# Moving a 32-byte constant and widening another so that SBUF buffers start on 64-byte lines

## The chip, the cores and the metric

The kernel runs on one core of one Trainium2 chip. The metric is device time in microseconds (us) from one launch; smaller is better. A core has a matrix engine (PE in the profile, with its weight loads shown as PEld), a vector engine (DVE), a scalar engine (ACT), a general engine (POOL) and a queue engine that issues most transfers (SP). On-chip data lie in SBUF, 128 partitions with the same layout in each, so an address here is a byte offset within a partition. Sums of matrix products lie in PSUM.

## The reference

The reference is a two-layer block for a latent generator: 512 latent tokens and 256 context tokens, model width 1024, 16 heads of 64. Every layer is a mixer and then a SwiGLU feed-forward network of hidden width 2816, each behind an RMS norm whose shift, scale and gate come from a conditioning vector.

```python
for l in range(DEPTH):                      # DEPTH = 2
    mx = (s_c @ mod_w[l] + mod_b[l]); mc = (s_cc @ mod_w[l] + mod_b[l])   # 6 vectors each
    hx = _rms(x, norm_mix_w[l]) * (1.0 + scx1) + shx1                     # the same for ctx
    if l % 2 == 0: ax, ac = _even_mixer(...)    # windowed and dense grouped-query attention
    else:          ax, ac = _odd_mixer(...)     # difference of two softmaxes per head
    x = x + gx1 * ax
    x = x + gx2 * _swiglu(_rms(x, norm_ffn_w[l]) * (1.0 + scx2) + shx2, ffn_w_in[l], ffn_w_out[l])
    # not in the last layer: the same two updates of ctx
return x
```

Everything is float32.

## The kernel before

**Arithmetic.** A large product of float32 matrices is made of three products of float32r operands: each operand is split into a rounded high part (a CAST on ACT, for instance L901) and a low part, the difference (a subtraction on DVE or POOL, for instance L911). High times high, high times low and low times high are summed in PSUM. A matrix multiplication on PE has a stationary operand of 128 columns, loaded first, and a moving operand of up to 512 columns that streams past it.

**Stages, in order.** The start loads modulation weights and makes the first norm (0 to 35 us). Layer 0's mixer follows: the input projection (`inps`, L466 to L468), scores (`sc`, L578), transposed probabilities (`ppt`, L612), values (`av`, L623) and the output projection (`ops`, L807 to L809). Layer 0's first feed-forward product (`p` and `pz`, L933) works on blocks of 384 tokens; its second one (`dps`, L1030 to L1032) has 512 moving columns. Layer 1 has the same shape with other attention lines (L715, L716, L734, L744), its feed-forward product works on blocks of 256 tokens, also on L933, and its second one is L1076 to L1078. The modulation sums of later parts run between the products of layer 0's feed-forward network (`modrow` L245, `modcol` L252).

**What the feed-forward product on L933 does.** The weights are the stationary operand (`wbh`, `wbl`) and the tokens the moving one. It is a block scheme with seven products a step, each of 12 matmuls. The moving blocks are `hT` (B11, B21), `b` (B12, B22, T4), `t` (T1, T3) and `hTt` (T2).

**Order.** From the sixth attention step of layer 0 on, PE's order is the one written in the source (`manual_schedule`); the other engines' orders, and PE's before that step, are laid out by a planner that simulates the program's time.

**Where buffers lie.** Pools stack up in SBUF from two ends, the left (low addresses) and the right (the top). Each tile's size is rounded up to a multiple of 32 bytes. In the allocation that the program before carries:

| side | first address, in bytes | pools |
|---|---|---|
| left | 16,512 (a multiple of 64) | cp (constants), keep, small, start, mix0, odd0, even0, blk0, rawh0, mods0, out0, state0 to 2, mix1, hid_low, hid_high, ring1, hop1, tmp1, g2 |
| right | top at 229,344 (32 past a multiple of 64) | mw0, w0, opa, blkt0, ring0, tmp0, mods1, wt, whi, wlo, mw1, w1 |

In `cp`, the tile `cst` has 262 columns of 4 bytes, 1,048 bytes, which occupy 1,056 (16.5 times 64). So `identr`, `identb`, `maskb` and `neghalf` behind it begin 32 bytes past a multiple of 64; `neghalf` has 32 bytes, and from `cols` on the left side is on multiples of 64 again. Only tiles of a few bytes in `small`, in `cp`'s tail and `negsink` fall on odd multiples of 32 there. On the right every size is a multiple of 64, so with the top 32 past a line every right tile begins 32 bytes past one.

A tile that begins on a multiple of 64 is called even in this document, one that begins 32 bytes behind it odd. The large operands are then:

| matmuls | moving | stationary |
|---|---|---|
| `inps` L466 to L468 | `wih`, `wil`, `wihi`, `wilo` in mw0, whi, wlo: odd | `hT`, `hTc` in keep: even |
| `sc` L578, L715, L716 | `kT` in even0, odd0, state: even | `qt`: even |
| `ops` L807 to L809 | `woh`, `wol` and most `wo` in w0, w1: odd; `wo` in keep: even | `hT`, `hTc`: even |
| layer 0, L933 | `hT`, `b`, `hTt`: even; `t` in blkt0: odd | `wbh`, `wbl` in ring0: odd |
| layer 0, L1030 to L1032 | even | even |
| layer 1, L933 and L1076 to L1078 | even | even |

The lines that the change touches are these:

```python
C_N = C_S4 + 4                                            # L42
cp = es.enter_context(tc.tile_pool(name="cp", bufs=1))    # L71
neghalf = cp.tile([P, 8], F32, name="neghalf")            # L139
```

`cst` is loaded once, by the first transfer of the queue (L121). `neghalf` is the exponent of the reciprocal square roots on POOL (L160), of at most 5 columns, and the input of two activations (L1360, L1740).

Of the kernel before, what the change touches and what calls it, by code (L numbers as in the profile page):

```python
# [11 lines left out]
F32 = mybir.dt.float32  # L12
# [7 lines left out]
P = 128  # L20
# [18 lines left out]
LAM_INIT = 0.8 - 0.6 * math.exp(-0.3)  # L39

C_ID, C_S2, C_ONE, C_S4 = 0, 128, 130, 258
C_N = C_S4 + 4  # L42


def swap_pairs(ap):
# [18 lines left out]
def backbone(es: ExitStack, tc: tile.TileContext, x, c, ctx, c_ctx, mod_w, mod_b, norm_mix_w, norm_ffn_w,  # L64
# [3 lines left out]
    nc = tc.nc  # L68
    PSUM = bass.MemoryType.PSUM

    cp = es.enter_context(tc.tile_pool(name="cp", bufs=1))  # L71
    keep = es.enter_context(tc.tile_pool(name="keep", bufs=1))
    small = es.enter_context(tc.tile_pool(name="small", bufs=6))
    dram = es.enter_context(tc.tile_pool(name="dram", bufs=1, space=bass.MemoryType.DRAM))
# [44 lines left out]

    cst = cp.tile([P, C_N], F32, name="cst")  # L120
    nc.sync.dma_start(cst, consts)  # L121
# [14 lines left out]
    mk = start.pool.tile([P, 2, P], F32, name="mk")  # L136
    nc.scalar.dma_start(mk, masks)
    nc.scalar.copy(maskb, mk)
    neghalf = cp.tile([P, 8], F32, name="neghalf")  # L139
    nc.gpsimd.memset(neghalf, -0.5)  # L140

    nc.scalar.activation(rows[0:16, :], rows[0:16, :], AF.Silu)
# [1105 lines left out]
    if True:  # L1248
        for i, (b, t) in enumerate(steps):
# [11 lines left out]
            if b < 3:  # L1261
                n = QUARTS[b][j]
# [571 lines left out]
def _constants():  # L1834
    k = np.zeros((P, C_N), np.float32)
    p = np.arange(P)
    k[:, C_ID:C_ID + P] = np.eye(P)
    k[:, C_S2] = p % 32 == 0
    k[:, C_S2 + 1] = p % 32 == 1
    k[:, C_ONE:C_ONE + P] = 1.0  # L1840
    k[:, C_S4:] = p[:, None] == 32 * np.arange(4)
    t = np.arange(SEQ)
    nf = HD // 4
    inv = np.float32(THETA) ** (-np.arange(nf, dtype=np.float32) / np.float32(nf))
    ang = np.concatenate([(t // GRID_W).astype(np.float32)[:, None] * inv,
                          (t % GRID_W).astype(np.float32)[:, None] * inv], axis=-1).astype(np.float32)
    cos, sin = np.cos(ang), np.sin(ang)
    r = np.empty((SEQ, 2, HD), np.float32)
    r[:, 0] = np.repeat(cos, 2, axis=-1)
    r[:, 1, 0::2] = -sin  # L1850
    r[:, 1, 1::2] = sin
    r = np.ascontiguousarray(r.reshape(NTX, P, 2, HD).transpose(1, 0, 2, 3))
    m = np.empty((P, 2, P), np.float32)
    m[:, 0] = np.where(p[None, :] >= p[:, None], 0.0, NEG)
    m[:, 1] = np.where(p[None, :] <= p[:, None], 0.0, NEG)
    return {"consts": k, "masks": m, "rope": r}
# [31 lines left out]
```

## Time and profile before

| what | value |
|---|---|
| median of 3 runs | 1697.88 us (1696.89 to 1704.94) |
| the profiled execution's own time | 1699.53 us |
| its span, first to last instruction | 1697.7 us |
| PE busy, share of the span | 1638.4 us, 97% |
| mean granted clock of PE | 0.993 |
| DVE, ACT, POOL busy | 1145.6, 939.1, 700.8 us |

The page gives busy time by engine and by line. The view of instructions in order of time gives a start and a length for each matmul. Matmuls overlap, and their ends are modelled, so what one costs in a full stream is the distance from its start to the next one's start, and not the length shown.

### The profile page before, as it was taken

The page shows a single profiled execution, that of the slowest core. Times are in us where ns is not written, and L with a number is a line of the kernel's source. Part 1 is how long each engine was busy: PE and PEld are TensorE (multiplying, and loading weights), DVE is VectorE, ACT ScalarE, POOL GpSimd, SP SyncE. Part 2 cuts the span into 40 slices and gives each one's busy share as a digit, 9 for nine tenths or more (in the row PEclk, how much of TensorE's full clock was granted, in tenths as well). Part 3 has the DMA queues.
Part 4 walks back from the last instruction along what each step waited for, and adds up shares of the span by engine and source line. Part 5 has one row for each costly group of instructions (what it writes and reads, how often), then busy time and mean ns, then how long its engine had stood idle before and what let it go on. Part 6 is the DMA issues. An engine that isn't in the chain of part 4 may idle for free. (4 is left out here: it accounts for less than half of the span.)

```text
span 1697.7 us, 28553 instructions
## 1 busy us (share of the span) xinstructions
PE 1638.4 (97%) x10378; PEld 1474.3 (87%) x10378; DVE 1145.6 (67%) x2012; ACT 939.1 (55%) x2011; POOL 700.8 (41%) x867
## 2 busy tenths in 40 slices
PE   6999999899999999999999989999999999999998
PEld 3977777677999999998777889999988899999887
DVE  3765656744899887767767656666666598887433
ACT  5565565745455665545564456666666555555321
POOL 2765554311345554402413366666664242221000
PEclk8999999999999999999999999999999999999999
DMA  9222221511455554439955311111112433331431
GB/s 323 65 71 75 69 69 50 180 45 48 120 168 174 171 158 150 136 115 330 309 185 177 104 41 38 48 44 42 46 47 99 122 91 106 107 106 57 137 98 63
DMA packets 217964, 194.64 MB, mean 115 GB/s; under 512 B 20000, under 2 KB 202592, under 8 KB 217824
## 3 DMA queue, kind: packets, MB, share of 16 engines
q1 hardware_dynamic: 217472, 192.62, 36.8%
q8 instruction: 81, 1.33, 0.3%
q14 instruction: 59, 0.48, 0.1%
q10 hardware_dynamic: 352, 0.21, 0.0%
HBM read 179.91 MB, written 12.87 MB: 114 GB/s over the span
## 5 line engine op out<-in xcount | busy, mean ns | idle before, releaser
L901 ACT CAST wbh<-wr 128x512 fp32r<-128x512 f32 x170 | 104.7, 621 | 139.2 <-PE p L933 76.0
L933 PE MATMUL p<-hT,wbh 128*128 128x256 f32 (+1 forms) x752 | 154.8, 299 | 0.0
L911 POOL TENSOR_TENSOR wbl<-wr,wbh 128x512 fp32r<-128x512 f32 x43 | 58.7, 1365 | 174.8 <-ACT wbh L901 174.8
L933 PEld LDWEIGHTS p<-hT,wbh 128*128 128x128 f32 x752 | 121.9, 191 | 0.2
L911 DVE TENSOR_TENSOR wbl<-wr,wbh 128x512 fp32r<-128x512 f32 x127 | 105.9, 842 | 22.9 <-ACT wbh L901 19.6
L933 PE MATMUL p<-hT,wbl 128*128 128x256 f32 (+1 forms) x376 | 112.1, 298 | 0.0
L933 PE MATMUL p<-t,wbh 128*128 128x384 f32 (+1 forms) x480 | 111.0, 317 | 0.0
L604 POOL TENSOR_SCALAR Pt<-Pt,rc 128x256 f32<-128x256 f32 (+3 forms) x96 | 73.3, 776 | 87.6 <-DVE rc L601 80.1
L231 POOL TENSOR_TENSOR modp<-modp 128x512 f32<-128x512 f32 x40 | 57.0, 1424 | 120.4 <-ACT modp L230 112.8
L933 PE MATMUL p<-hTt,wbh 128*128 128x256 f32 (+1 forms) x480 | 101.3, 303 | 0.0
L887 POOL TENSOR_TENSOR wr<-wr 128x512 f32<-128x512 f32 x40 | 61.7, 1543 | 85.3 <-DVE ws L892 84.3
L466 PE MATMUL inps<-wih,hT 128*128 128x384 f32 x256 | 90.6, 354 | 6.4 <-ACT qkv L677 6.4
L933 PE MATMUL p<-b,wbh 128*128 128x384 f32 x368 | 94.7, 339 | 0.3 <-DVE c L961 0.3
L901 ACT CAST wbh<-ws 128x512 fp32r<-128x512 f32 x120 | 69.6, 581 | 42.0 <-PE p L933 29.1
L224 DVE SCALAR_TENSOR_TENSOR ma<-modw,cols,ma 128x256 f32<-128x256 f32 x140 | 86.3, 617 | 2.3
L592 ACT ACTIVATE Pt<-sc,nm 128x256 f32<-128x256 f32 (+3 forms) x96 | 67.8, 709 | 35.1 <-DVE nm L588 19.1
L468 PE MATMUL inps<-wih,hT 128*128 128x384 f32 x256 | 86.7, 339 | 0.0
L467 PE MATMUL inps<-wil,hT 128*128 128x384 f32 x256 | 86.5, 338 | 0.0
L911 DVE TENSOR_TENSOR wbl<-ws,wbh 128x512 fp32r<-128x512 f32 x120 | 81.6, 680 | 2.1 <-ACT wbh L901 2.0
L933 PEld LDWEIGHTS p<-t,wbh 128*128 128x128 f32 x480 | 82.9, 189 | 0.0
L933 PEld LDWEIGHTS p<-hTt,wbh 128*128 128x128 f32 x480 | 78.4, 191 | 3.1 <-ACT modp L230 2.1
L230 ACT ACTIVATE modp<-modw,cols 128x256 f32<-128x256 f32 x160 | 68.4, 500 | 15.6 <-DMA modw<-in_mod_w_dram 7.7
(355 smaller groups left out, 5378.8 us busy)
## 6 DMA issues: line engine op xcount, KB each, us to landing
modw<-in_mod_w_dram SPq DMA_DIRECT2D x96, 512.0 KB, 4.5
wr<-in_ffn_w_in_dram SPq DMA_DIRECT2D x176, 256.0 KB, 3.4
wdr<-in_ffn_w_out_dram SPq DMA_DIRECT2D x66, 512.0 KB, 3.7
wir<-in_od_w_in_dram SPq DMA_DIRECT2D x96, 128.0 KB, 2.3
hidm<-hid SPq DMA_DIRECT2D x44, 192.0 KB, 1.9
hr<-hidm SPq DMA_DIRECT2D x22, 192.0 KB, 3.4
x<-in_x_dram SPq DMA_DIRECT2D x8, 512.0 KB, 6.1
wir<-in_ev_w_in_dram SPq DMA_DIRECT2D x16, 256.0 KB
```

Of the source, the lines that this page charges most:

```text
L224: nc.vector.scalar_tensor_tensor(acc, w[:, k], scale[k], acc, ALU.mult, ALU.add)
L230: nc.scalar.activation(pr[:, k], w[:, k], AF.Copy, scale=scale[k])
L231: nc.gpsimd.tensor_add(pr[:, 0:2], pr[:, 0:2], pr[:, 2:4])
L466: nc.tensor.matmul(ps, hs[0][:, k, :], a, start=k == 0, stop=False)
L467: nc.tensor.matmul(ps, hs[0][:, k, :], b, start=False, stop=False)
L468: nc.tensor.matmul(ps, hs[1][:, k, :], a, start=False, stop=k == KT - 1)
L592: turn["exp"] = nc.scalar.activation(p[:, :n], s, AF.Exp, bias=nm[:, c1], accum_out=sm[:, c1])
L604: nc.gpsimd.tensor_scalar(p[:, :n], p[:, :n], rc[:, hh:hh + 1], 1.0, ALU.mult, ALU.mult)
L887: nc.gpsimd.tensor_sub(w, raw[f, "G1"], w)
L901: nc.scalar.copy(hi, w)
L911: (nc.gpsimd if name == "G2" else nc.vector).tensor_sub(lo, raw[need[n]], f32(hi))
L933: nc.tensor.matmul(ps, w[:, k, :], H[b][h][:, k, :], start=first and k == 0 and q == 0, stop=final and k == 3 and q == 2, skip_group_check ...
```

## The change

`cst` gets eight more columns of zeros (its rows go from 1,048 to 1,080 bytes, which occupy 1,088, 17 times 64), and `neghalf` goes into a pool of its own, `edge`, which is opened first on the right side and so takes the top 32 bytes. The left side from `cols` on stays where it was, since 32 bytes come and 32 go; `identr`, `identb` and `maskb` move up by 32 to a multiple of 64. The right side's pools all move down by 32, to multiples of 64. No instruction is added, removed or given another shape but the load of `cst`.

```diff
 C_ID, C_S2, C_ONE, C_S4 = 0, 128, 130, 258
-C_N = C_S4 + 4
+C_N = C_S4 + 12
...
-    cp = es.enter_context(tc.tile_pool(name="cp", bufs=1))
+    cp, edge = (es.enter_context(tc.tile_pool(name=n, bufs=1, side=s)) for n, s in (("cp", "left"), ("edge", "right")))
...
-    neghalf = cp.tile([P, 8], F32, name="neghalf")
+    neghalf = edge.tile([P, 8], F32, name="neghalf")
     nc.gpsimd.memset(neghalf, -0.5)
...
-    k[:, C_S4:] = p[:, None] == 32 * np.arange(4)
+    k[:, C_S4:C_S4 + 4] = p[:, None] == 32 * np.arange(4)
```

## The prediction

> **What bounds the kernel now.** I read the page's busy times first, then the busy time of each engine by stage, then the instructions of PE in order of time, and the chain that ended last.
>
> ```profile
> span 1697.7 us, 28553 instructions
> PE 1638.4 (97%) x10378; PEld 1474.3 (87%) x10378; DVE 1145.6 (67%) x2012; ACT 939.1 (55%) x2011; POOL 700.8 (41%) x867
> ```
>
> ```profile
> 100.00:410.00 310.00, 294.89 (x2049) 234.29 (x2049) 187.51 (x399) 182.02 (x430) 133.63 (x198) 0.99 0.25 78
> 410.00:840.00 430.00, 429.22 (x2386) 407.21 (x2385) 341.12 (x544) 236.85 (x461) 178.39 (x143) 1.00 0.57 176
> 1000.00:1270.00 270.00, 262.33 (x1813) 251.65 (x1812) 171.85 (x350) 174.86 (x452) 180.55 (x285) 1.00 0.14 42
> 1348.00:1573.00 225.00, 225.00 (x1877) 224.94 (x1876) 190.31 (x284) 127.43 (x245) 63.78 (x45) 1.00 0.34 97
> ```
>
> The second fence has, for a stretch of time, its length and the busy time of PE, weight loads, DVE, ACT and POOL, then the granted clock. PE bounds every large stage: it idles 0.8 of 430 us in layer 0's feed-forward part, nothing in layer 1's, 7.7 of 270 us in layer 1's mixer and 15 of 310 us in layer 0's. So only what shortens PE's stream counts, and the question is what an address has to do with the distance between two matmuls.
>
> **Where PE's distance depends on parity.** A full stream is seen best where all buffers are even, in layer 1's feed-forward product:
>
> ```profile
> 1376.16 1.44 PE pz L933 x12
> 1377.60 8.64 PE p L933 x72
> 1386.24 1.44 PE pz L933 x12
> ```
>
> 72 matmuls of 256 columns take 8.64 us, 120.0 ns each. In layer 0 the same line has 384 columns; its stationary `wbh` and `wbl` are odd, its moving blocks even except `t`:
>
> ```profile
> 605.80 0.51 PE L933 MATMUL p<-b,wbh 128*128 128x384 f32 x2
> 607.36 0.51 PE L933 MATMUL p<-t,wbh 128*128 128x384 f32 x2
> 609.27 0.34 PE L933 MATMUL p<-t,wbl 128*128 128x384 f32 x1
> 609.44 0.50 PE L252 MATMUL modcol<-cst,ma 128*128 128x4 f32 x4
> 614.05 0.52 PE L933 MATMUL p<-b,wbh 128*128 128x384 f32 x2
> 616.17 0.52 PE L933 MATMUL p<-hTt,wbh 128*128 128x384 f32 x2
> ```
>
> From 605.80 to 607.36 lie nine matmuls: 173.3 ns each. From 607.36 to 609.27, on `t`, eleven: 173.6. But from 614.05, right behind another `t` block, twelve matmuls on the same `b` take 2.12 us, 176.7 each. The first pace is the full one: 173.3 minus 120.0 over 128 columns is 0.417 ns a column, which leaves 13.3 ns a matmul and gives 226.7 for 512 columns. The second is 3.4 ns slower, and stays so until something else breaks the stream. I followed all even-moving stretches of this product by their starts. 32 begin right behind a `t` block, and every one is slow; 20 begin elsewhere (behind modulation matmuls, at the product's start), and none is. The first and the last slow one:
>
> ```profile
> 464.25 0.34 PE L933 MATMUL p<-hTt,wbh 128*128 128x384 f32 x1
> 470.62 0.51 PE L933 MATMUL p<-t,wbh 128*128 128x384 f32 x2
> ...
> 750.21 0.52 PE L933 MATMUL p<-b,wbh 128*128 128x384 f32 x2
> 752.33 0.27 PE L288 MATMUL gps<-cst,modc 128*8 128x128 f32 x1
> ```
>
> They are 36 matmuls in 6.37 us (176.9) and 12 in 2.12 (176.7). The other two products of mixed parity have an odd moving and an even stationary operand:
>
> ```profile
> 1053.04 0.34 PE L466 MATMUL inps<-wih,hT 128*128 128x384 f32 x1
> 1055.16 0.27 PE L734 MATMUL ppt<-cst,e 128*128 128x128 f32 x1
> ```
>
> ```profile
> 360.90 0.39 PE L807 MATMUL ops<-woh,hT 128*128 128x512 f32 x1
> 366.27 0.40 PE L809 MATMUL ops<-woh,hT 128*128 128x512 f32 x1
> ```
>
> `inps`: twelve in 2.12 us, 176.7 against 173.3. `ops`: 23 in 5.37 us, 233.5 against 226.7, 6.8 too many, and no faster at the end than at the start. An all-even product of 512 columns that is entered badly recovers:
>
> ```profile
> 904.62 0.40 PE L1030 MATMUL dps<-wdh,hdh 128*128 128x512 f32 x1
> 906.47 0.39 PE L1032 MATMUL dps<-wdh,hdl 128*128 128x512 f32 x1
> 908.50 0.39 PE L1032 MATMUL dps<-wdh,hdl 128*128 128x512 f32 x1
> ```
>
> Eight matmuls at 231, then nine at 226. My reading: where moving and stationary operand have the same parity (`t` with `wbh`, all of layer 1's product, `dps`) PE falls into the full pace; where they differ, a slow pace, once entered, lasts.
>
> **The change, part by part.** All these operands become even, so the slow pace should go.
>
> ```profile
> L466 PE MATMUL inps<-wih,hT 128*128 128x384 f32 x256 | 90.6, 354 | 6.4 <-ACT qkv L677 6.4
> L466 PE MATMUL inps<-wihi,hT 128*128 128x384 f32 x128 | 47.1, 368 | 0.3 <-ACT qkv L520 0.3
> L466 PE MATMUL inps<-wihi,hTc 128*128 128x384 f32 x64 | 23.3, 364 | 1.1 <-ACT qkv L520 1.1
> L807 PE MATMUL ops<-wo,hT 128*128 128x512 f32 x64 | 26.5, 413 | 0.0
> L807 PE MATMUL ops<-woh,hT 128*128 128x512 f32 x64 | 25.5, 398 | 0.0
> L807 PE MATMUL ops<-woh,hTc 128*128 128x512 f32 x32 | 12.8, 401 | 0.0
> ```
>
> Layer 0's product: 780 of its matmuls lie in the 32 slow stretches; times 3.4 ns is 2.7 us. The ceiling is all 1,344 even-moving ones, 4.6. The stage is full of PE, so all of it counts. It waits for no transfer there, so where those land in SBUF is hidden.
>
> `inps`: 448 on L466 and as many on L467 and L468, 1,344 times 3.4 is 4.6 us. What stays is a bad entry, some 112 of them (one for each 12). A `dps` entry costs 8 times 4.6 ns, 36 ns; half of that for 384 columns leaves 2.0 us, while the clean entries behind modulation matmuls leave nothing. I take 1.0, so 3.6 saved.
>
> `ops`: 160 on each of three lines; 72 of the 480 have the even `wo` in `keep`. 408 times 6.8 is 2.8 us; 20 entries of 36 ns stay, 0.7, so 2.1 saved.
>
> The last two stand in the mixers, where PE idles 3 to 5% and waits for ACT's copies (first row above); I count 90%, 5.1 us of 5.7.
>
> The other operands. The scores' 192 or so matmuls of 512 columns are even already, but run between `inps` blocks; they may start cleaner, 0 to 6.8 ns each, 0 to 1.3 us; I take 0.4, as they are runs of four, shorter than the recovery seen. The 368 float32r transposes (`identr`, `qd`, `kd`) go from two odd operands to two even ones; by `t` against layer 1 that is nothing, and I allow 0.4 us of at most 1.3 (3.4 ns each). The load of `cst` grows by 4 KB, 0.013 us at the 324 GB/s of the start:
>
> ```profile
> 0.00:35.00 35.00, 20.89 (x154) 12.46 (x154) 11.34 (x27) 20.60 (x39) 6.71 (x19) 0.95 0.98 324
> ```
>
> For ACT, DVE and POOL nothing: the same cast on odd buffers (layer 0) and on even ones (layer 1) takes the same time, and what they gain or lose hides behind PE in both stages.
>
> ```profile
> L901 ACT CAST wbh<-wr 128x512 fp32r<-128x512 f32 x86 | 53.0, 621 | 87.1 <-PE p L933 46.2 <-issue 38.8 <-DMA wr<-in_ffn_w_in_dram 1.5
> ...
> L901 ACT CAST wbh<-wr 128x512 fp32r<-128x512 f32 x84 | 51.7, 620 | 52.1 <-PE p L933 29.8 <-PE pz L933 11.2 <-ACT s L938 11.1
> ```
>
> `neghalf`, 32 bytes, is written and read as before. No wait is added: a tile waits for earlier ones in its place, and after the move the pairs that share an address are those of before, less three that shared 32 bytes and whose first tile was long dead.
>
> Sum: 2.7 + 5.1 + 0.4 + 0.4 = 8.6 us. The profiled execution took 1699.53 us with 1.8 outside its span; the median of the runs is 1697.88. From the median, 1689.3; from the profiled execution, 1690.9.
>
> [...]
>
> **The rivals.** *No change.* The slow pace could hang on something that goes with the order, the size of matmul before or the PSUM bank, and not on parity. For it: the scores are even and not at the full pace. Against it: 32 of 32 and 0 of 20, with the same operands. Time 1697.9.
>
> *More.* Every entry becomes clean as well: 2.7 + 4.6 + 2.8 + 1.3 + 1.3 is 12.7 us, 1685.2. For it: entries behind modulation matmuls are clean. Against it: `dps` at 904.62 is even and enters badly.
>
> *Slower.* The planner lays out ACT, DVE, POOL and the queue by simulated time, and `cst`'s load is the first event. If it moves one of ACT's copies behind a cast at every head of layer 1, PE waits there:
>
> ```profile
> PE inps L466 <- ACT qkv L677: 4.3, 8, 1.3
> ```
>
> That is eight waits and 4.3 us now. Four more such sums eat the gain and make 17 us, from which it would be over 0.5% slower, 1706.4. Against it: nothing in an engine's work changes, and 4 KB shift all events alike.
>
> **How the numbers follow.** The forecast, a gain of 4.5 to 11 us around 8.6, has 0.74, half of it above 8.5 us (0.5% of 1697.88, about what a measurement of this kernel can tell from no change). More has 0.11, no change 0.08, slower 0.07. Faster by over 0.5% is then 0.37 + 0.11, 0.48; within 0.5% is 0.37 + 0.08, 0.45; slower 0.07. The forecast's own range is 1687 to 1693; with More at the low end and a mixer that gives back most of its share at the high one (2.7 us of the first part alone gives 1695.2), 1684.5 to 1695.5 holds 0.8.
>
> **What would show it.** In the view of instructions in order of time, `b` and `hTt` behind `t` at 173.3 ns and not 176.7; twelve `inps` in 2.08 us; `ops` behind its first eight at 226.7; layer 0's feed-forward part 2.7 us shorter, layer 1's unchanged. It is wrong if those distances stay, if the orders of ACT or POOL differ, or if PE's waits grow by what its stream loses.

## The result, and the profile after

The kernel after takes 1695.45 us (median of 22 runs, 1691.36 to 1698.70), the kernel before 1699.44 us over 22 runs beside it (1694.96 to 1704.94). The ratio is 0.9974, with a 95% interval of 0.9966 to 0.9983: a gain of 4.4 us, between 2.9 and 5.8 (the two medians lie 4.0 apart). The forecast was a gain of 8.6, in a range of 4.5 to 11. The direction was right; what was measured is half of what was forecast, just under that range. The change stays within the 0.5% that the prediction took for what a measurement can tell, but over 22 runs the interval is only 0.09% to either side and leaves no change out.

The page of the kernel after, its span and its line of busy times:

```profile
span 1690.7 us, 28553 instructions
PE 1628.1 (96%) x10378; PEld 1465.3 (87%) x10378; DVE 1143.5 (68%) x2012; ACT 938.4 (56%) x2011; POOL 695.1 (41%) x867
```

This profiled execution took 1692.5 us, that of before 1699.53. Their difference, 7.0 us, is more than the medians show: the execution of after lies 3 us below its own median, that of before at its median. Part of it is therefore not the change's. The mean granted clock, 0.993 before and 0.995 after, stands for some 3.4 us of it, an estimate (0.7% of 1697.7 us less 0.5% of 1690.7; in before, where the clock is 0.50 from 1272.6 us on for 3.4 us, two scores of 512 columns start 0.43 us apart, and 0.24 behind it). The same instructions stand in the same order on every engine as before, so stages can be compared one by one.

The busy time by stage of the kernel after (length, then PE, weight loads, DVE, ACT and POOL, then the granted clock):

```profile
100.00:410.00 310.00, 293.99 (x2061) 234.17 (x2060) 189.30 (x403) 182.22 (x431) 134.45 (x201) 1.00 0.25 79
410.00:840.00 430.00, 429.02 (x2391) 407.05 (x2390) 340.58 (x546) 238.55 (x463) 183.37 (x145) 1.00 0.57 179
1000.00:1270.00 270.00, 260.78 (x1827) 249.91 (x1826) 173.91 (x353) 176.62 (x458) 178.44 (x286) 1.00 0.15 44
1348.00:1573.00 225.00, 225.00 (x1851) 223.78 (x1850) 192.87 (x285) 127.16 (x244) 61.59 (x42) 1.00 0.34 99
```

PE still fills both feed-forward parts (429.02 of 430 us, 225.00 of 225). In layer 1's mixer, though, it now idles 9.2 of 270 us (7.7 before), and in layer 0's 16.0 of 310 (15.1 before): part of what PE's stream gave up there has come back as waiting.

What became of the stretches behind `t` shows in the instructions in order of time, of the kernel after:

```profile
612.58 0.51 PE L933 MATMUL p<-t,wbh 128*128 128x384 f32 x2
...
613.10 0.50 PE L933 MATMUL p<-b,wbh 128*128 128x384 f32 x2
...
615.17 0.51 PE L933 MATMUL p<-hTt,wbh 128*128 128x384 f32 x2
```

Twelve matmuls on `b` behind a `t` block take 2.07 us, 172.5 ns each, where they took 176.7: the slow pace that the prediction rests on is gone there. But another has appeared. Behind a modulation sum, before and after:

```profile
508.67 0.64 PE L245 MATMUL modrow<-ma,cst 128*32 128x256 f32 x8
...
511.42 0.51 PE L933 MATMUL pz<-hT,wbh 128*128 128x384 f32 x2
...
513.50 0.51 PE L933 MATMUL p<-b,wbh 128*128 128x384 f32 x2
...
515.58 0.34 PE L933 MATMUL p<-t,wbh 128*128 128x384 f32 x1
```

```profile
508.13 0.64 PE L245 MATMUL modrow<-ma,cst 128*32 128x256 f32 x8
...
510.90 0.51 PE L933 MATMUL pz<-hT,wbh 128*128 128x384 f32 x2
...
513.00 0.51 PE L933 MATMUL p<-b,wbh 128*128 128x384 f32 x2
...
515.10 0.51 PE L933 MATMUL p<-t,wbh 128*128 128x384 f32 x2
```

From 511.42 to 515.58 lie 24 matmuls before, 4.16 us, 173.3 ns each; from 510.90 to 515.10 the same 24 after, 4.20 us, 175.0. These stretches were clean before. Counted as unbroken runs of even-moving matmuls, 19 stretches of this product don't begin behind `t` (20 by the prediction's count), and all are clean before. In after, the seven behind `modrow` are slow by 1.3 ns a matmul, the three behind the transposes `gps` by 3.5, and the two at the product's start by 1.8 and 2.8; the seven behind `modcol` stay clean.

`inps` and `ops` of the kernel after (one mixed block each; the rows between are left out):

```profile
1056.64 0.34 PE L467 MATMUL inps<-wil,hT 128*128 128x384 f32 x1
...
1058.55 0.47 PE L696 MATMUL qpt<-identr,qd 128*128 128x128 f32 x4
```

```profile
361.07 0.40 PE L807 MATMUL ops<-woh,hT 128*128 128x512 f32 x1
...
366.34 0.39 PE L809 MATMUL ops<-woh,hT 128*128 128x512 f32 x1
```

Eleven `inps` take 1.91 us, 173.6 ns each (176.7 before). 23 `ops` take 5.27 us, 229.1 (233.5 before, 226.7 forecast). And PE's wait at the head of the `inps` blocks, in the view of waits of the kernel after (microseconds, times, longest):

```profile
PE inps L466 <- ACT qkv L677: 8.6, 11, 1.4
```

It was 7.2 over the same 11 times.

**Stages over all traces.** Since one trace holds some microseconds of chance, I measured four stages in the traces of every kernel below that computes the block, from the first matmul of one stage to the first of the next. For the kernels before and after, the rows that bound layer 0's `ops` and feed-forward stages:

```profile
332.44 0.40 PE L807 MATMUL ops<-woh,hT 128*128 128x512 f32 x1
...
425.89 0.33 PE L933 MATMUL p<-hT 128*128 128x384 f32 x1
...
763.46 0.40 PE L1030 MATMUL dps<-hT,hTt 128*128 128x512 f32 x1
```

```profile
332.86 0.39 PE L807 MATMUL ops<-woh,hT 128*128 128x512 f32 x1
...
425.45 0.34 PE L933 MATMUL p<-hT 128*128 128x384 f32 x1
...
761.88 0.39 PE L1030 MATMUL dps<-hT,hTt 128*128 128x512 f32 x1
```

The table gives them all, under the names of the experiments below. "Distance" is the place of the large right-hand tiles minus that of the left-hand ones, modulo 128 bytes, in `inps` and in the other two; it turned out to be the better name for what is varied than even and odd.

| kernel | distance (`inps`; `ops` and L933) | layer 0's mixer, `sc` to `ops` | `ops` stage, layer 0 | L933, layer 0 | layer 1's mixer, `sc` to `ops` |
|---|---|---|---|---|---|
| before | 96; 96 | 259.61 | 93.46 | 337.57 | 265.03 |
| e2 | 96; 96 | 258.60 | 93.42 | 337.99 | 264.86 |
| d1 | 64; 96 | 262.34 | 93.44 | 338.61 | 263.32 |
| d2 | 96; 64 | 260.30 | 92.61 | 336.18 | 265.48 |
| after | 64; 64 | 258.46 | 92.59 | 336.43 | 263.58 |
| after again (f2) | 64; 64 | 258.74 | 92.59 | 336.22 | 264.04 |
| e1 | 64; 64 | 261.01 | 92.53 | 337.05 | 264.12 |
| b1 | 64; 0 | 259.75 | 92.21 | 335.47 | 263.75 |
| e3 | 0; 0 | 258.30 | 92.19 | 335.03 | 263.36 |
| f1 | 32; 32 | 258.79 | 93.40 | 337.19 | 264.55 |

Between distances 96 and 64, the means of the kernels of each kind differ by 0.9 us in the `ops` stage (93.44 against 92.58), 1.6 in layer 0's feed-forward product (338.06 against 336.47) and 1.4 in layer 1's mixer (265.12 against 263.76, by `inps`). Together 3.9 us, which accounts for the 4.4 that were timed, within its interval. In layer 0's mixer the kinds don't part: the spread is 4 us, the means are 259.5 and 260.1. Part of that spread goes with the granted clock. In before it falls to 0.50 from 197.4 us on for 3.4 us, which costs 1.7 us, an estimate (half of the 3.4). Over 100 to 410 us, which hold most of this stage, its mean is 0.99 in d1, e1, d2 and before, four of the five longest, and 1.00 in b1, after, f2, f1 and e3. Among the five shortest, e2 at distance 96 takes 258.60 us, after and f2 at 64 take 258.46 and 258.74: no gain that can be told, though the distances between the starts of `inps` in this stage sum to 1.0 us less in after than in before. PE idles 16.1 us of the stage in e2, and 16.7 and 17.0 in after and f2, so 0.6 to 0.8 us of that has come back as waiting.

Layer 0's second feed-forward product, whose operands lie on one side and keep their distance, took 192.04 us before and 189.65 after, but also 189.28 in e2 and 192.45 in f2 (whose mean granted clock was 0.992 over the whole execution, against 0.995 in after and 0.997 in e2). It doesn't part by distance either.

### The profile page after: what moved, and what is told of

It reads as the page before. It is cut to its first block, busy times and chain, and to the rows that moved or that the text cites. A ratio compares the mean times of both kernels' runs of the same rounds, so it can differ in the third digit from the quotient of the medians.

```text
span 1690.7 us, 28553 instructions
## 1 busy us (share of the span) xinstructions
PE 1628.1 (96%) x10378; PEld 1465.3 (87%) x10378; DVE 1143.5 (68%) x2012; ACT 938.4 (56%) x2011; POOL 695.1 (41%) x867
## 5 line engine op out<-in xcount | busy, mean ns | idle before, releaser
L933 PE MATMUL p<-hT,wbh 128*128 128x256 f32 (+1 forms) x752 | 154.4, 299 | 0.0
L933 PEld LDWEIGHTS p<-hT,wbh 128*128 128x128 f32 x752 | 121.9, 191 | 0.2
L933 PE MATMUL p<-hT,wbl 128*128 128x256 f32 (+1 forms) x376 | 111.9, 298 | 0.0
L933 PE MATMUL p<-t,wbh 128*128 128x384 f32 (+1 forms) x480 | 111.3, 318 | 0.0
L933 PE MATMUL p<-hTt,wbh 128*128 128x256 f32 (+1 forms) x480 | 101.0, 303 | 0.0
L933 PE MATMUL p<-b,wbh 128*128 128x384 f32 x368 | 93.8, 336 | 0.4 <-DVE c L961 0.4
L933 PEld LDWEIGHTS p<-t,wbh 128*128 128x128 f32 x480 | 82.9, 189 | 0.0
L933 PEld LDWEIGHTS p<-hTt,wbh 128*128 128x128 f32 x480 | 78.3, 191 | 3.1 <-ACT modp L230 2.1
```

Source lines behind the costliest of these rows:

```text
L933: nc.tensor.matmul(ps, w[:, k, :], H[b][h][:, k, :], start=first and k == 0 and q == 0, stop=final and k == 3 and q == 2, skip_group_check ...
```

## The experiments

The theory at the start was the prediction's: moving and stationary operands of the same parity, modulo 64 bytes, fall into the full pace, and where they differ a slow pace lasts. Against it stood that a place on a multiple of 64 bytes itself matters, for any reader or writer of a buffer (the title and the expectations call such a place a 64-byte line; no run shows that the hardware has lines), and later that the pace goes by the distance of the two sides beyond their parity, and by what ran before. Each kernel below was timed beside the kernel before; the two of bare streams are read from their traces alone.

**Lines or pairs: e1_all_odd.** The left side is moved onto the odd places of the right; nothing large begins on a multiple of 64 bytes, and all pairs match.

```diff
-C_N = C_S4 + 4
+C_N = C_S4 + 12
...
-    k[:, C_S4:] = p[:, None] == 32 * np.arange(4)
+    k[:, C_S4:C_S4 + 4] = p[:, None] == 32 * np.arange(4)
```

> The constants' tile is widened by eight columns and the small constant stays on the left behind it, so nearly every large tile of both sides begins 32 bytes past a 64-byte line: all odd, and the moving and the stationary operand of every large product agree. Pair theory (the pace depends on whether the two agree): like the changed kernel, 0.997 of the kernel before, inps at 173 to 174 ns. Line theory (an operand off its 64-byte line is read slowly): no better than the kernel before, 1.000 or more, since layer 1's feed-forward product becomes odd too, and its 72 matmuls take more than 8.64 us.

Measured: 0.9981 (0.9971 to 0.9991), 1696.61 us. Its `b` block behind `t`, in order of time:

```profile
615.89 0.50 PE L933 MATMUL p<-b,wbh 128*128 128x384 f32 x2
...
617.97 0.51 PE L933 MATMUL p<-hTt,wbh 128*128 128x384 f32 x2
```

Twelve in 2.08 us, 173.3 ns, with no large tile on a multiple of 64. Its wait for `qkv` on L677 is the longer one of the kernel after, too (8.5 us). It gains as the change does, within the intervals, so that a buffer begins on a multiple of 64 is not the cause. What the two kernels share is the distance between the two sides.

**e2_left_odd.** The right side is on multiples of 64 as after, the left one is shifted off them.

```diff
-    cp = es.enter_context(tc.tile_pool(name="cp", bufs=1))
+    cp, edge = (es.enter_context(tc.tile_pool(name=n, bufs=1, side=s)) for n, s in (("cp", "left"), ("edge", "right")))
...
-    neghalf = cp.tile([P, 8], F32, name="neghalf")
+    neghalf = edge.tile([P, 8], F32, name="neghalf")
```

> The small constant goes to the top of the right side, the constants' tile stays narrow: the left side from the columns' tile on is odd, the right side even, so the operands disagree as in the kernel before, with the sides swapped. Pair theory: 1.000 of the kernel before, inps at 176 to 177 ns. Line theory: the odd operands are now the tokens; inps and ops, whose moving operand becomes even, gain (0.998), the layer 0 feed-forward product, whose moving blocks become odd but for t, does not.

Measured: 1.0002 (0.9991 to 1.0013), 1699.11 us. An `inps` block of its trace:

```profile
1050.03 0.34 PE L466 MATMUL inps<-wih,hT 128*128 128x384 f32 x1
...
1052.15 0.82 PE L734 MATMUL ppt<-cst,e 128*128 128x128 f32 x6
```

Twelve in 2.12 us, 176.7 ns, as before. Here `neghalf` and all large tiles moved, the right ones onto multiples of 64, and nothing changed: both sides moved by the same 32 bytes. So e1 and e2 show from both sides that it is the relative place.

**e3_right_128.** As after, with the right side another 64 bytes lower, on multiples of 128. Parity modulo 64 is that of after.

```diff
-    neghalf = edge.tile([P, 8], F32, name="neghalf")
+    neghalf = edge.tile([P, 24], F32, name="neghalf")[:, 0:8]
```

> The changed kernel with the small constant's tile 64 bytes larger, so that the right side begins on multiples of 128 and not 64 behind one; the left side as in the changed kernel. If only 64-byte parity counts: as the changed kernel, 0.997, and the layer 0 feed-forward product keeps its excess of 0.8 ns a matmul. If what is left of the slow pace there and in ops is a matter of 128 bytes: 2 to 3 us less than the changed kernel, 0.996.

Measured: 0.9972 (0.9961 to 0.9982), 1695.21 us; a total that can't be told from after's, but not the same streams. Layer 0's product is 1.4 us shorter than in after (335.03 against 336.43), and its excess over the full pace, summed over the starts of its matmuls of 384 columns, is 0.31 us against 1.56 in after and 2.79 before. `inps` goes the other way: 1.41 us of excess, against 0.23 in after (nothing, if steps under 170 ns are counted too) and 3.50 before. So the place modulo 64 bytes doesn't settle the pace; it counts modulo 128 at least, and more wasn't tried.

**The law by itself: m1_grid.** 24 matmuls in a stream, for each combination of parities, directly behind transposes or sums, or with a first block of twelve of each combination in between. E and O are the parities of the moving and of the stationary operand.

```diff
...
+        for N, nm, br in ((384, "t", turn_break), (384, "s", sum_break), (512, "w", turn_break), (256, "n", turn_break)):
+            for e in (None, "EE", "EO", "OE", "OO"):
+                for d in ("EE", "EO", "OE", "OO"):
+                    br()
+                    if e:
+                        block(f"{nm}in_{e}_{d}", "in", e, N, 12)
+                    last = block(f"{nm}_{e or 'XX'}_{d}", "body", d, N, 24)
...
```

> Not the block at all: streams of 24 float32r matmuls of 384, 512 and 256 columns with every parity of moving and stationary operand (E even, O odd; the first letter is the moving one), each behind a break of four float32 transposes or four modulation sums, and behind no entry or an entry of 12 matmuls of another parity. The output is not the block's. Pair theory: 24 matmuls of 384 columns take 24 x 173.3 = 4.16 us in EE and OO whatever the entry, and 24 x 176.7 = 4.24 us in EO and OE behind an entry of the other moving parity. Line theory: only bodies with an odd moving operand are slow. History alone: the body's pace follows the entry's or the break's kind, not its own parity.

Three of the four combinations behind four transposes, in order of time (24 matmuls each, to the start of the next transposes):

```profile
10.08 4.52 PE L95 MATMUL t_XX_EE<-mv,st 128*128 128x384 f32 x24
14.43 0.60 PE L102 MATMUL brt<-cst,raw 128*128 128x128 f32 x4
14.79 4.42 PE L95 MATMUL t_XX_EO<-mv,st 128*128 128x384 f32 x24
19.04 0.60 PE L102 MATMUL brt<-cst,raw 128*128 128x128 f32 x4
...
24.01 4.49 PE L95 MATMUL t_XX_OO<-mv,st 128*128 128x384 f32 x24
28.34 0.60 PE L102 MATMUL brt<-cst,raw 128*128 128x128 f32 x4
```

The totals mislead here. EE's 4.35 us come from its first step alone, 369 ns from the first start to the second, where the others have 259 to 262; its last eleven distances are 173.3 ns each. So are those of EO and OE, which take 4.25 and 4.26 us. OO (4.33 us) stays slow to its end, 176.7 ns. Over all 40 streams of 384 columns, behind transposes or sums and with or without a first block of twelve, the last eleven distances are at the full pace in all 20 of mixed parity, and 0.9 to 3.4 ns slow in 11 of the 20 of the same parity: against the prediction's rule. Put as distances, moving minus stationary, EE and OO are both at 64 here, EO at 32 and OE at 96. So it isn't the block's `inps` either, which is slow at 96, and as EE and OO behind the same transposes differ (173.3 and 176.7 ns), the distance alone is no law. With 512 columns every combination was 6.4 to 7.9 ns slow against 226.7, which is the prediction's estimate from 120.0 and 173.3. As a law of pairs the prediction's reading is wrong; in the block it described what this arrangement does.

**Part by part: d1_inps_even and d2_ffn_ops_even.** The kernel before, with 32 bytes of padding on the right only while the weights of `inps` are there, or only while those of layer 0's `ops` and feed-forward products and layer 1's `ops` are there.

```diff
...
+        pad = Pool("pad", "right")
+        pad.pool.tile([P, 8], F32, name="pad")
...
+        pad.close()
...
```

> The kernel before with 32 bytes taken from the top of the right side while mw0, and while wlo, whi, wt, mods1 and mw1 are open: only the operands of inps become even; ops and the layer 0 feed-forward product stay mixed. If the three parts add up: inps at 173.5 ns and not 176.6, 2 to 3.5 us less than the kernel before (0.998 to 0.9987), layer 0's feed-forward stage as before (337.4 us), its matmuls behind t slow. If the mixers give back what their stream loses: 0.9995 or more.

> The kernel before with the 32 bytes taken only while w0, opa, blkt0, ring0, tmp0 and w1 are open: the complement, ops and the layer 0 feed-forward product become even, inps stays mixed. If the parts add up: layer 0's feed-forward stage 1.1 us shorter, ops 1.5 us, 2 to 2.7 us in all (0.9984 to 0.9988), and the gains of this kernel and of the one with inps alone even add up to that of the changed kernel (0.9974).

Measured: 0.9991 (0.9980 to 1.0002) for `inps` alone, 0.9981 (0.9969 to 0.9993) for the others alone. The two gains add to 0.28%, that of the change is 0.26%: the parts add up as far as intervals of 0.11 and 0.12% to either side can tell, and d1's own reaches no change. The stages say the same: d1 has after's layer 1 mixer (263.32) and before's other two stages, d2 the reverse. The waits, of d1 and then of d2:

```profile
PE inps L466 <- ACT qkv L677: 8.2, 11, 1.4
```

```profile
PE inps L466 <- ACT qkv L677: 7.1, 11, 1.3
```

In the three kernels with `inps` at distance 96 this wait sums to 7.0 to 7.2 us, in the five at distance 64 to 8.1 to 8.6. That is 1.2 us given back at one wait. It fits PE arriving earlier at a copy of `qkv` out of PSUM that ACT ends when it did; the ends of the copies were not compared.

**b1_offsets.** After, with 64 bytes more of padding in d2's places: `inps` stays at 64, where its excess was 0.23 us in after (1.41 at 0 in e3), and the others go to 0, where layer 0's product had 0.31 us in e3 (1.56 in after).

```diff
...
+                pad = Pool("pad", "right")
+                pad.pool.tile([P, 16], F32, name="pad")
...
+        pad.close()
...
```

> The changed kernel with 64 bytes more taken from the right while w0, opa, blkt0, ring0, tmp0 and w1 are open: inps stays 64 bytes past a multiple of 128, where its excess was 0.2 ns; ops and the layer 0 feed-forward product go to multiples of 128, where theirs were 1.4 and 0.2 ns instead of 3.2 and 0.8. If the pace follows the distance of the two operands modulo 128 bytes: 1.2 us less in that product, 0.8 us in ops, 0.996 of the kernel before, and below the changed kernel. If what is left there is chance: as the changed kernel.

Measured: 0.9972 (0.9959 to 0.9985), 1695.04 us. It has the least excess of all, the three streams taken together (0.35 us in layer 0's product, 0.25 in `inps`, 0.66 in `ops`). One `ops` block:

```profile
362.90 0.39 PE L807 MATMUL ops<-woh,hT 128*128 128x512 f32 x1
...
368.13 0.39 PE L809 MATMUL ops<-woh,hT 128*128 128x512 f32 x1
```

23 in 5.23 us, 227.4 ns, near the 226.7 that the prediction estimated as the full pace. Beside after's 0.9974, the 0.9972 is no gain that these runs can tell: the two stages are 1.3 us shorter together, and the interval is 2.2 us wide to either side.

**The three streams by themselves: m2_offsets.** Streams in the order and with the shapes of the block's products, the right-hand buffers at 0, 32, 64 and 96 bytes past the left ones (names `za` to `zd`).

```diff
...
+            seq = ("hA", "tA", "bA", "hB", "hC", "bB", "tB")
+            where = {"h": (h, 0, 512, 4096), "b": (b, 0, 384, 1536), "t": (t, r, 384, 1536)}
+            for part in range(3):
+                if part != 2:
+                    sum_break()
+                for i, s in enumerate(seq):
...
+                    last = product(f"{m}{'uvw'[part]}{s}", r, *where[s[0]])
...
```

> Not the block: the streams of the layer 0 feed-forward product (h, t, b, h, h, b, t behind a break of four modulation sums), of inps and of ops, with the left buffers fixed and the right ones 0, 32, 64 or 96 bytes further, twice over. The output is not the block's. The kernel before has 96, the changed one 64, the one with the right side on multiples of 128 has 0. Pair theory by 64 bytes: 0 and 64 at full pace (173.3, 226.7), 32 and 96 slow behind t, in inps and in ops. By 128 bytes: 0 and 64 differ as the two kernels do: the feed-forward stream behind the sums at 174.5 ns for 64 and 173.5 for 0, ops at 230 and 228.

Two blocks for each distance, in order of time (each row has twelve matmuls and begins where the one above ends), first 0, then 32, 64 and 96:

```profile
62.97 2.28 PE L102 MATMUL zawhC<-h,w 128*128 128x384 f32 x12
65.09 2.27 PE L102 MATMUL zawbB<-b,w 128*128 128x384 f32 x12
...
100.12 2.28 PE L102 MATMUL zbuhC<-h,w 128*128 128x384 f32 x12
102.24 2.28 PE L102 MATMUL zbubB<-b,w 128*128 128x384 f32 x12
...
168.40 2.24 PE L102 MATMUL zcuhC<-h,w 128*128 128x384 f32 x12
170.48 2.24 PE L102 MATMUL zcubB<-b,w 128*128 128x384 f32 x12
...
236.21 2.28 PE L102 MATMUL zduhC<-h,w 128*128 128x384 f32 x12
238.33 2.28 PE L102 MATMUL zdubB<-b,w 128*128 128x384 f32 x12
```

2.12 us (176.7 ns each) at 0, at 32 and at 96, and 2.08 (173.3) at 64: of these blocks only those at 64 are at full pace. `inps` was full at 0, 32 and 64 (24 matmuls in 4.24 to 4.25 us) and 3.4 ns slow at 96 (4.32 and 4.33 us); `ops` was 5.6 to 7.6 ns slow against 226.7 at all four. For 96 this rebuilds the kernel before in detail: `h` ahead of the first `t` is clean, and of the blocks of `h` and `b` behind it all but one in each of two passes are slow. For 64 it agrees with `b` behind `t` in after. But at 0 it says slow where the block is fastest (`b` behind `t` in e3, from 611.57 us on: twelve in 2.08 us), and it doesn't have after's slow pace behind the sums.

**f1_distance_32.** The one distance not yet tried in the block. The right side goes down by 64 bytes and stays odd, so that by the prediction's parities nothing changes.

```diff
+    es.enter_context(tc.tile_pool(name="edge", bufs=1, side="right")).tile([P, 16], F32, name="pad")
```

> The kernel before with 64 bytes taken from the top of the right side at the start: the right side stays odd, so every pair of operands differs in parity as before, but the right operands now lie 32 bytes past the left ones modulo 128, where they lay 96 past. Theory of 64-byte parity: nothing changes, inps at 176.6 ns, 1.000. Theory of the distance modulo 128 bytes, from the streams run alone: inps goes to the full pace (173.4), the layer 0 feed-forward product becomes slow in all of its stretches (2.7 to 3.3 ns, 5 to 6 us where it was 2.8), ops from 6.9 to 7.6; 1 to 2 us more in all, 1.001.

Measured: 0.9989 (0.9977 to 1.0001), 1697.50 us. The total can't be told from no change, but the streams can. In order of time, a `b` block behind `t`, then two `inps` blocks (lines are one higher in this kernel):

```profile
614.20 0.51 PE L934 MATMUL p<-b,wbh 128*128 128x384 f32 x2
...
616.29 0.51 PE L934 MATMUL p<-hTt,wbh 128*128 128x384 f32 x2
```

```profile
1052.66 0.34 PE L467 MATMUL inps<-wih,hT 128*128 128x384 f32 x1
...
1054.79 0.82 PE L735 MATMUL ppt<-cst,e 128*128 128x128 f32 x6
...
1056.32 0.33 PE L468 MATMUL inps<-wil,hT 128*128 128x384 f32 x1
...
1058.23 1.50 PE L745 MATMUL av<-vv,PT 128*128 128x128 f32 x12
```

`b` behind `t` takes 2.09 us and not 2.12, though the pair differs in parity. Of the two `inps` blocks, entered behind scores twelve take 2.13 us (177.5 ns each), entered behind a wait eleven take 1.91 (173.6): operands at the same distance at both paces, by what came before. Parity modulo 64 falls as the rule, and m2's streams forecast this kernel only in part (slow everywhere in layer 0's product, which had 1.78 us of excess against before's 2.79; slower in `ops`, whose stage kept its 93.40 us; full pace in `inps`, which has both).

**f2_after_again.** The kernel after once more, with no edit.

> The changed kernel once more, beside the one above: 0.9974 of the kernel before; stage by stage as in its first trace, 92.6 us for the stage of layer 0's ops, 336.3 for the layer 0 feed-forward product, 263.6 from the first scores of layer 1 to its ops. Where its first trace differed by chance (the second product of layer 0, 189.7 us), it should not repeat.

Measured: 0.9973 (0.9963 to 0.9983), 1695.17 us. The ratio repeats; in its trace the three stages repeat within 0.5 us, and layer 0's second product doesn't (192.45 us against 189.65). With e2's 189.28 at the distances of before, that is why the 2.4 us of the first pair of traces are not put down to the change.

## Why the prediction was right, and where it was wrong

*Right: that it is PE's stream, that addresses decide its pace, and that it is the relative place of the two operands.* e1 and e2 show it from both sides: with no large tile on a multiple of 64 the gain is there (twelve on `b` behind `t` in 2.08 us, 173.3 ns each), with the right side on multiples of 64 and the left shifted along it is not (twelve `inps` in 2.12 us, 176.7).

*Right: no change of order, and nothing on ACT, DVE, POOL or the queue that bears on PE.* POOL's busy time, 695.1 us against 700.8, varies between 693.5 and 702.0 over the kernels of the table. The slower rival, by the planner, falls with that. No change falls too: the ratio was 0.9974 (0.9966 to 0.9983).

*Wrong, the step that failed: "where moving and stationary operand have the same parity ... PE falls into the full pace".* The 32 slow stretches against 20 clean ones were all from one arrangement, with one distance for every mixed pair. The rule fitted them, but so would any rule that sets distance 96 apart from distance 0, and `dps`, the only witness for same parity with 512 columns, is at distance 0, not at after's 64. What the runs put in its place: in the block the pace goes by the distance, modulo 128 at least (layer 0's product has 2.79 us of excess at 96, 1.78 at 32, 1.56 at 64 and 0.31 at 0), and by the stream before. At 64 the 32 stretches behind `t` become full (173.3 ns), and 12 of 19 others become slow, by 1.3 to 3.5 ns. *A second step failed with it: "I count 90%" for the mixers.* Of the 4.7 us of the sum that aren't seen, 1.8 are `inps` time that no stage shows, 1.1 are missing in layer 0's product, 1.0 in `ops`, and 0.8 in the scores and transposes. By terms:

- Layer 0's product: 2.7 us forecast, 1.6 in the stages' means (1.2 in the sum over starts: 2.79 to 1.56 us). The 2.7 was there to be had: at distance 0 the stage is 2.8 shorter than at 96.
- `inps`: 3.6 us of stream forecast, 3.3 measured with 384 columns (3.50 to 0.23), so this term was right as a stream. What became of it was mis-sized: 90% was counted, and 1.4 us show in layer 1's mixer and none in layer 0's. 1.2 us are shown to come back at the wait for ACT's `qkv` on L677. Of the stream's gain, 1.0 us lies in layer 0's mixer, and 0.6 to 0.8 of it are seen again as idle time of PE there; which of its waits grew was not settled. Some 0.4 us in each layer lies ahead of the first scores, outside the stages of the table.
- `ops`: 2.1 us of stream forecast, counted at 90%. The sum over starts gives 1.5 (2.8 to 1.3), of which 1.1 lie in layer 0 and 0.4 in layer 1. Layer 0's stage is 0.9 us shorter; layer 1's was not told from its spread. "An all-even product of 512 columns that is entered badly recovers" was read from `dps` and failed for `ops`: the blocks still run at 229.1 ns where 226.7 was forecast. `dps` itself is at distance 0, and at 0 `ops` comes to 227.4 (b1).
- Scores, 0.4: nothing. Their excess is 0.99 us before and 1.02 after. Transposes, 0.4: nothing seen.

The sum of what is seen is 3.9 of 8.6 us, and the median fell by 4.4. The rival in which every entry becomes clean falls too: b1 comes nearest to it and doesn't beat after by anything measurable.

What stays open is the law itself. Distance and history both enter: m2's blocks took 2.12 us at 96 and 2.08 at 64, and f1's `inps` ran at 177.5 and at 173.6 ns at one distance; and m2 forecasts some blocks and fails at others. Nor is the distance enough: m1's EE and OO share it and differ (173.3 and 176.7 ns). Which property of the addresses or of the preceding instructions carries the history wasn't found, and distances beyond 128 bytes weren't told apart. The stationary operands' weight loads overlap these streams (in before they are busy for 407.21 and PE for 429.22 of the 430 us from 410 us on), and they were not varied apart from the matmuls.

## What to carry to other kernels

In these streams, which PE bounds, the relative place of the moving and the stationary buffers, to 32 bytes, was worth 2 or 3% of a matmul's time (176.7 ns at distance 96 against 173.3 at 64, 233.5 at 96 against 227.4 at 0). In another kernel, shift one side by 32, 64 and 96 bytes in each phase and measure, rather than align everything. Look at distances between starts, not at the lengths shown, and don't make a law from one arrangement, however many stretches fit it: vary the arrangement first, in a bare stream and then in the kernel, since here the two didn't agree (at distance 0, twelve on `b` behind `t` took 2.08 us in e3, and the `b` block of m2's fence 2.12). Where PE waits for another engine at the head of each block, count back what that wait will take (1.2 us here), and before a difference of 2 us between two traces is given a cause, compare their granted clock stage by stage and profile more than once.

## What the runs showed of the hardware

The same matmul of float32r has more than two paces in a steady stream, by addresses and by what ran before: 173.3, 175.0 and 176.7 ns with 384 columns, 227.4, 229.1 and 233.5 with 512 (means over blocks). Nor is the "full pace" of the prediction a floor. With 256 columns it gave 120.0 ns; in the kernel after, a block of `inps` on `hTc` shows less:

```profile
1140.28 0.28 PE L466 MATMUL inps<-wih,hTc 128*128 128x256 f32 x1
...
1141.57 0.28 PE L468 MATMUL inps<-wih,hTc 128*128 128x256 f32 x1
```

Eleven distances in 1.29 us, 117.3 ns each. And a bare stream of m1, of even operands behind twelve others of its kind, shows less again:

```profile
448.49 2.89 PE L95 MATMUL n_EE_EE<-mv,st 128*128 128x256 f32 x24
451.21 0.60 PE L102 MATMUL brt<-cst,raw 128*128 128x128 f32 x4
```

Here 24 matmuls take 2.72 us, 113.3 ns each. So with 256 columns 120.0, 117.3 and 113.3 ns were measured; what sets them apart was not found. The prediction's 226.7 ns for 512 columns is worked out from 120.0 and 173.3 and stays an estimate: nine of `dps` took 2.03 us in before, from 906.47 to 908.50, 225.6 each.
